# The end of a two-layer encoder: token tile 2 scaled by ScalarE and sent by an adding transfer, a smaller descriptor scratch, five loads on GpSimd's queue

## The chip, the cores and the metric

The kernel runs on one core of one Trainium2 chip, as one program. The metric is the device time of one execution in microseconds (us), lower is better. The engines are called as in the profile: PE (TensorE), DVE (VectorE), ACT (ScalarE), POOL (GpSimd) and SP (SyncE, which here only issues transfers). 16 DMA engines move data; two queues feed them, one issued by SyncE and one by GpSimd.

## The reference

Two layers (DEPTH = 2) over 512 tokens of width 1024, all in float32. Each layer has a token part (a 2-D neighbourhood attention, a bidirectional retention, gates) and a channel part; the end of the program is the end of the second layer's channel part:

```python
for i in range(DEPTH):
    proj = x @ w_in[i]
    q_na, k_na, v_na, q_r, k_r, v_r, g_r, gate_a, gate_b = jnp.split(proj, IN_SPLITS, axis=-1)
    ya = neighbourhood_attention(q_na, k_na, v_na, na_rpb[i])
    yb = bidirectional_retention(q_r, k_r, v_r, g_r, ret_decay_f[i], ret_decay_b[i])
    merged = jax.nn.sigmoid(gate_a) * (ya @ w_branch_a[i]) + jax.nn.sigmoid(gate_b) * (yb @ w_branch_b[i])
    x = layer_norm(DEEPNORM_ALPHA * x + merged @ w_out[i], ln1_g[i], ln1_b[i])
    ffn = conv_glu_ffn(x, w_up[i], conv_w[i], conv_b[i], w_down[i])      # (gelu(a) * b) @ w_down
    ple = jax.nn.sigmoid(x @ w_ple_gate[i]) * (p[i] @ w_ple_proj[i])
    x = layer_norm(DEEPNORM_ALPHA * x + ffn + ple, ln2_g[i], ln2_b[i])

def layer_norm(x, g, b):
    mu, var = mean(x), mean(square(x - mu))          # over the 1024 channels
    return (x - mu) * lax.rsqrt(var + LN_EPS) * g + b
```

## The kernel before

**Precision and weights.** Every matrix product is made of three products of float32r parts (`hi` and `lo` of each operand: `hi*hi`, `hi*lo`, `lo*hi`, in `mm3`). Weights lie in HBM as chunks of 128 x 1024 and pass through one stream (`Stream`): a load into `raw` on SyncE's queue, a cast to `hi` on ScalarE and a subtraction to `lo` on VectorE (`split`), a few chunks ahead of TensorE. Many products are block products in which seven products (`a`, `c`, `t1`, `t2`, `d`, `t3`, `t4`, a Strassen form) replace eight; their weight sums are formed in memory by adding transfers on GpSimd's queue (`Stream.add`, a DMA with `accum_op=add`, into the tiles `rawa` and `rawt`). GpSimd does little else.

**Order.** Nearly everything is kept in the order in which the program is written, on every engine and queue. The stream of a layer is written out by hand: `VG0` and `VG1` are the orders of the first part of layer 0 and 1 (two blocks of retention values and gates, `0a` to `0t4` and `1a` to `1t4`, with the chunks `ga0` to `ga5` of one gate between them), then `FILL` (the heads' `q`, `k`, `nq`, `nk` and others, among them the blocks `2a`, `3a`, `2c`, `3c` at its start), between which the steps of the retention and attention heads are placed. In layer 0, the loads of five constant tables (`cos_sb`, `sin_sb`, `xi_sb`, `dist_sb`, `ident`) are issued at the entry `0t4`, and those of the mask, the bias windows and the convolution weights at `1t4` (`TABLES_AT`). `q_head` (in `FILL`) uses `dist_sb` and `xi_sb` first, in `decays` (L791 to L795).

**Channel part and end.** `pg` forms the gated per-layer input and begins the up-projection; then three segments (`SEGS = (3, 4, 4)`) follow, each with its up-tiles (`up_step`) and the block product of the down-projection. In the last segment of layer 1 (`fin and last`) the layer norm and the output lie between the products. The four token tiles `R[0]` to `R[3]` (128 tokens x 1024) take different ways out:

- Tiles 0 and 1: `out` is filled ahead of time with the layer norm's `b` (a transfer that repeats one row of `ln_par`, on SyncE's queue, before the channel part), and the tile, times `g` and the reciprocal deviation, is added to it in memory by an adding transfer on GpSimd's queue (`send`). Tile 0 is scaled by ScalarE and multiplied by `g` on GpSimd (`norm_gb`), tile 1 by VectorE and ScalarE (`norm_g`, `norm_gs`).
- Tiles 2 and 3: `norm_g` and `norm_b`, both on VectorE, the second with `b` from SBUF (`lnb`), then plain transfers on SyncE's queue; tile 3 goes in two halves of 512 channels.

The reciprocal deviation comes from GpSimd (`rstd_of`, a power), but for tile 3, where ScalarE takes a square root and VectorE and ScalarE make one Newton step (`refine`), so that no engine has to wait for GpSimd. All engines' operations here are in the order of the program: `product("t3")`, the copies `w` of its two results by ScalarE, the ways out of tiles 0 and 1, the additions `into` tiles 2 and 3, `product("t4")` with tile 2's half first, the moments of tiles 2 and 3, `norm_g(2)`, and at last

```python
                if last:
                    norm_b(2, (slice(0, 1024),))
                    refine(3)
                    norm_g(3)
                    norm_b(3, (N1, N2))
```

`unit_f` and `unit_r` take tiles out of one pool of 27 buffers of 4 KB a partition; a tile waits until an earlier one in its buffer is done with. `g` and `b` of the last layer norm (`lng`, `lnb`, by `ln_consts`) are two of them.

Of the kernel before, what the change touches and what calls it, by code (L numbers as in the profile page):

```python
# [10 lines left out]
AF = mybir.ActivationFunctionType  # L11
ALU = mybir.AluOpType
AX = mybir.AxisListType

P = 128
D = 1024
# [5 lines left out]
LN_EPS = 1e-5  # L22
# [3 lines left out]
RPB_N = 8 * 15 * 31  # L26

N_UNIT = 27
N_RAW = 3
N_W = 3  # L30
N_TMP = 6
# [5 lines left out]
XT_HELD = (("t3",), ("t3", "t4"))  # L37
DEEP = 5

FILL = ('2a', '3a', '2c', '3c', 'q0', '2t1', '3t1', 'k0', '2t2', '2d', '3d', '3t2', '2t3', '3t3', '2t4', '3t4', 'k1', 'q1', 'nq0', 'k2', 'nk0', 'q2', 'nk1', 'q3', 'k3', 'nq1', 'nq3', 'nq2', 'nk2', 'nk3', 'vn', 'bb0', 'bb1', 'bb2', 'ga6', 'bb3', 'ga7', 'bb4', 'bb5', 'bb6', 'bb7', 'xn')  # L40
# [5 lines left out]
VG0 = ('p0', 'p1', '0a', '0c', '1a', '1c', 'ga0', '0t1', 'ga1', '0t2', 'ga2', '0d', '0t3', '1t1', '0t4', 'ga3', '1t2', 'ga4', '1d', '1t3', 'ga5', '1t4')  # L46
# [56 lines left out]
def trunk(tc, wpack, x_nat, x_tr, head, p_tr, rpb, decay, ln_par, ln_col, conv, cos_t, sin_t, dist, xi_d, zd, mask, ident_d, out):  # L103
    nc = _Engines(tc)
# [3 lines left out]
    with ExitStack() as es:  # L108
        pool = lambda name, bufs, **k: es.enter_context(tc.tile_pool(name=name, bufs=bufs, **k))
        cp = pool("const", 1)  # L110
        up = pool("unit", N_UNIT)
        xp = pool("xt", 1)
        rp = pool("raw", N_RAW)
        wp = pool("wsplit", N_W)
# [24 lines left out]
        def small(s, n):  # L139
            return sp.tile([P, n], F32, tag=f"s{n}", name=nm(s))  # L140
# [77 lines left out]
        def fill_items(l):  # L218
            by = {}

            for b in range(2, 4):
                pos = {(q, 0): (l, 36 + 4 * (b - 2) + i, 0, 1024) for i, q in enumerate("acbd")}
                for it in block_items(pos, {}, VG_EARLY, 1):
                    by[f"{b}{it.kind}"] = [it]
            return [it for k in FILL for it in (by[k] if k in by else plain_items(l, k))]

# [214 lines left out]
                s3 = ps.rearrange("p (k c) -> p k c", c=P)  # L441
                split(xt[:, 4 * h:4 * h + 4, 0, t * P:(t + 1) * P], xt[:, 4 * h:4 * h + 4, 1, t * P:(t + 1) * P], s3)

        def ln_consts(l, which):
            g = unit_f("lng")
            b = unit_f("lnb")
            nc.sync.dma_start(g, ln_par[l, 2 * which:2 * which + 1, :].to_broadcast([P, D]))
            nc.sync.dma_start(b, ln_par[l, 2 * which + 1:2 * which + 2, :].to_broadcast([P, D]))
            return g, b

        def ln_tile(z, st, g, b, parts):
# [62 lines left out]
        p0 = ws.seq[0]  # L514
# [121 lines left out]
        for l in range(DEPTH):  # L636
# [258 lines left out]
            qn, kn, kl, vn = {}, {}, {}, {}  # L895
# [125 lines left out]
            xn = []  # L1021
# [44 lines left out]
            u, v, keep = {}, {}, {}  # L1066
# [101 lines left out]
            for m in range(8):  # L1168
# [12 lines left out]
                u = unit_r("mt")  # L1181
# [34 lines left out]
            last = l == DEPTH - 1  # L1216

            _Ordered.on = set(ORD)

            if last:  # L1220

                for t in range(2):
                    nc.sync.dma_start(out[t * P:(t + 1) * P, :], ln_par[l, 3:4, :].to_broadcast([P, D]))

            R = [unit_f("R") for _ in range(4)]
            for t in range(4):
                nc.sync.dma_start(R[t], rscr[l][t * P:(t + 1) * P, :])
# [18 lines left out]
            a11, k2, sa, sb, sums = {}, {}, {}, {}, []  # L1246
# [132 lines left out]
            pg()  # L1379
            st = [sp.tile([P, 2, 6], F32, tag="bn", name=nm("bn")) for _ in range(4)]  # L1380
            for s, n in enumerate(SEGS):
                for j in range(tile - 2 * sum(SEGS[:s]), 2 * n):
                    up_step(j, j == 2 * n - 1)
                    residual()
                fin = s == len(SEGS) - 1
# [39 lines left out]
                    if fin:  # L1425
                        nc.vector.bn_stats(st[t][:, cb, :], R[t][:, (N1, N2)[cb]])

                if fin and last:
                    g2c, b2c = ln_consts(l, 1)
                if fin and not last:  # L1430

                    gb = cp.tile([P, 2, 8], F32, name="gb")
# [2 lines left out]
                mv, rs, nmr = {}, {}, {}  # L1435

                def moments(t):
                    mv[t] = small("mv", 2)
                    nc.vector.bn_aggr(mv[t], st[t])
                    if fin and last and t == 3:  # L1440
                        ve[0] = small("ve", 1)
                        nc.vector.tensor_scalar_add(ve[0], mv[t][:, 1:2], LN_EPS)
                        ve[1] = small("sd", 1)
                        nc.scalar.activation(ve[1], ve[0], AF.Sqrt)
                        return
                    rs[t] = rstd_of(mv[t][:, 1:2], LN_EPS, 1)

                ve = {}

                def refine(t):  # L1450

                    r, a, rs[t] = (small(k, 1) for k in ("ri", "ra", "rstd"))
                    nc.vector.reciprocal(r, ve[1])
                    nc.vector.scalar_tensor_tensor(a, r, ve[0], r, op0=ALU.mult, op1=ALU.mult)
                    nc.scalar.activation(a, a, AF.Copy, scale=-0.5, bias=1.5)
                    nc.scalar.activation(rs[t], r, AF.Copy, scale=a)

# [79 lines left out]
                product("t3", u, False)  # L1537
                if fin and last:

                    nc.scalar.copy(w[0], u[0])  # L1540
                    norm_gb(0)
                    nc.scalar.copy(w[1], u[1])
                    norm_gs(1)
                    x4 = u
                elif fin:
                    for i in range(2):
                        norm(i)
                        nc.sync.dma_start(scr[i * P:(i + 1) * P, :], R[i])
# [12 lines left out]
                for k in BOUND if not last else ("t4a", "t4b"):  # L1561
                    if k[0] == "p":
                        ple_half(l + 1, int(k[1]))
                    elif k == "tr":
                        ws.xw = None
                        xt = xp.tile([P, 8, 2, 512], F32R, tag="xt", name=nm("xt"))
                        xf = {}
                        drain(out_pair(0, xt, xf))
                    else:
                        i = "ab".index(k[2]) + 2  # L1570
                        next(t4)
                        into(i, N1, x4[i - 2])
                        stats(i, 0)
                        moments(i)
                        if not last:
                            norm(i)
                            nc.sync.dma_start(scr[i * P:(i + 1) * P, :], R[i])
                        elif i == 2:
                            norm_g(2)
                if last:  # L1580
                    norm_b(2, (slice(0, 1024),))
                    refine(3)
                    norm_g(3)
                    norm_b(3, (N1, N2))
# [128 lines left out]
```

## Time and profile before

| | before |
|---|---|
| median of 3 runs | 1687.07 us |
| lowest, highest | 1686.46, 1687.68 us |
| the profiled execution: its own time | 1687.74 us |
| its span (first to last instruction) | 1686.0 us |
| granted TensorE clock | 0.998 |
| transfers, mean over the span | 170 GB/s |

The page of the profile gives busy time, share of the span and instructions of each engine, and the chain of waits that ended last. Rows of a timeline give start in us, duration in us, engine, line, operation, `out<-in` with the tile names, shape and count, and in brackets the idle time of the engine ahead of it with what ended it. Rows of DMA issues give the count, KB of each and the median time from issue to landing. `SPq` and `POOL ... DMA_DIRECT2D` are issues of transfers on SyncE's and GpSimd's queues. The first and last microseconds of the span are the program's start and its closing barrier.

### The profile page before, as it was taken

The page shows a single profiled execution, that of the slowest core. Times are in us where ns is not written, and L with a number is a line of the kernel's source. Part 1 is how long each engine was busy: PE and PEld are TensorE (multiplying, and loading weights), DVE is VectorE, ACT ScalarE, POOL GpSimd, SP SyncE. Part 2 cuts the span into 40 slices and gives each one's busy share as a digit, 9 for nine tenths or more (in the row PEclk, how much of TensorE's full clock was granted, in tenths as well). Part 3 has the DMA queues.
Part 4 walks back from the last instruction along what each step waited for, and adds up shares of the span by engine and source line. Part 5 has one row for each costly group of instructions (what it writes and reads, how often), then busy time and mean ns, then how long its engine had stood idle before and what let it go on. Part 6 is the DMA issues. An engine that isn't in the chain of part 4 may idle for free.

```text
span 1686.0 us, 21792 instructions
## 1 busy us (share of the span) xinstructions
PE 1672.7 (99%) x8183; PEld 1413.7 (84%) x8183; DVE 1218.7 (72%) x1848; ACT 935.7 (55%) x1400; POOL 177.9 (11%) x204
## 2 busy tenths in 40 slices
PE   9999999999999999999999999999999999999997
PEld 7889988888888888888888898888888888888885
DVE  6746777766787767767876467878588887676678
ACT  6755667773366435344476556586634574453453
POOL 1111111100200100000112011110002010000012
PEclk9999999999999999999999999999999999999999
DMA  8978665666755535536779677656767564274275
GB/s 302 262 190 224 160 145 129 174 175 218 207 137 162 122 113 160 139 105 177 201 221 224 167 201 166 142 129 159 209 245 203 130 168 120 87 200 114 87 212 100
DMA packets 85929, 285.99 MB, mean 170 GB/s; under 512 B 9920, under 2 KB 12480, under 8 KB 85824
## 3 DMA queue, kind: packets, MB, share of 16 engines
q1 hardware_dynamic: 61920, 199.66, 33.7%
q0 software_dynamic: 23904, 84.95, 29.1%
q8 instruction: 64, 1.05, 0.2%
q14 instruction: 41, 0.34, 0.1%
HBM read 265.69 MB, written 17.83 MB: 168 GB/s over the span
## 4 chain that ended last, share of the span: by engine, by line
PE 97%; DVE 1%; ACT 1%; issue 0%; DVEq 0%; ACTq 0%
PE gt L86 32%; PE u L86 13%; PE v L86 7%; PE gt L383 6%; PE gt L384 6%; PE gt L385 6%; PE w L86 4%; PE gn L385 2%; PE gn L383 2%; PE gn L384 2%; PE x L86 1%; PE gn L86 1%; PE u L385 1%; PE u L384 1%; PE u L383 1%; PE na L1005 1%
## 5 line engine op out<-in xcount | busy, mean ns | idle before, releaser
L86 PE MATMUL gt<-x1t,hi 128*128 128x512 f32 x1408 | 433.5, 389 | 0.0
L86 PEld LDWEIGHTS gt<-x1t,hi 128*128 128x128 f32 x1408 | 264.3, 188 | 54.9
L86 PE MATMUL gt<-x1t,lo 128*128 128x512 f32 x704 | 274.1, 389 | 0.1
L86 DVE TENSOR_TENSOR lo<-raw,hi 128x1024 fp32r<-128x1024 f32 (+1 forms) x152 | 181.9, 1207 | 44.4 <-ACT hi L86 44.3
L86 DVE SCALAR_TENSOR_TENSOR ca<-gt,cw,ca 128x511 f32<-128x511 f32 x176 | 131.8, 749 | 78.3 <-ACT ca L86 75.2
L86 ACT CAST hi<-raw 128x1024 fp32r<-128x1024 f32 (+1 forms) x152 | 156.2, 1037 | 36.0 <-PE x L86 11.3
L86 PEld LDWEIGHTS gt<-x1t,lo 128*128 128x128 f32 x704 | 132.1, 188 | 28.2 <-DVE lo L86 1.0
L86 DVE TENSOR_TENSOR lo<-rawa,hi 128x1024 fp32r<-128x1024 f32 x94 | 109.6, 1177 | 52.1 <-ACT hi L86 51.8
L86 ACT ACTIVATE ca<-gt,cw 128x512 f32<-128x512 f32 x88 | 68.5, 779 | 131.6 <-PE gt L86 131.6
L86 ACT CAST hi<-rawa 128x1024 fp32r<-128x1024 f32 x94 | 94.1, 1013 | 36.4 <-DMA rawa<-in_wpack 16.5
L383 PE MATMUL gt<-xt,hi 128*128 128x512 f32 x288 | 113.6, 394 | 0.0
L384 PE MATMUL gt<-xt,hi 128*128 128x512 f32 x288 | 112.3, 390 | 0.0
L385 PE MATMUL gt<-xt,lo 128*128 128x512 f32 x288 | 112.2, 390 | 0.0
L86 POOL DMA_DIRECT2D rawa<-in_wpack x72 | 64.4, 908 | 410.2 <-DVE lo L86 344.2
L341 ACT CAST hi<-raw 128x1024 fp32r<-128x1024 f32 x48 | 50.5, 1052 | 61.0 <-PE gt L384 55.5
L156 ACT CAST hi<-raw 128x1024 fp32r<-128x1024 f32 x43 | 44.9, 1050 | 64.9 <-PE gt L384 34.4
L343 POOL DMA_DIRECT2D lo<-in_wpack x48 | 42.2, 879 | 325.0 <-ACT lo L342 246.8
L157 DVE TENSOR_TENSOR lo<-raw,hi 128x1024 fp32r<-128x1024 f32 x43 | 52.3, 1222 | 16.9 <-ACT hi L156 16.3
L385 PEld LDWEIGHTS gt<-xt,lo 128*128 128x128 f32 x288 | 54.1, 188 | 11.6
L383 PEld LDWEIGHTS gt<-xt,hi 128*128 128x128 f32 x288 | 54.2, 188 | 10.1
L384 PEld LDWEIGHTS gt<-xt,hi 128*128 128x128 f32 x288 | 54.2, 188 | 10.0
L86 PE MATMUL gt<-xt,hi 128*128 128x512 f32 x192 | 59.1, 389 | 0.0
(349 smaller groups left out, 4030.7 us busy)
## 6 DMA issues: line engine op xcount, KB each, us to landing
raw<-in_wpack SPq DMA_DIRECT2D x239, 512.0 KB, 3.7
rawa<-in_wpack POOLq DMA_DIRECT2D x78, 512.0 KB, 6.5
lo<-in_wpack POOLq DMA_DIRECT2D x48, 512.0 KB, 5.5
rawa<-in_wpack SPq DMA_DIRECT2D x26, 512.0 KB, 6.5
rawt<-in_wpack SPq DMA_DIRECT2D x26, 512.0 KB, 6.6
rawt<-in_wpack POOLq DMA_DIRECT2D x26, 512.0 KB, 7.4
r_scr<-pp SPq DMA_DIRECT2D x8, 512.0 KB, 10.0
g_scr<-sga SPq DMA_DIRECT2D x16, 256.0 KB, 3.9
```

The lines of the kernel that those rows point to most:

```text
L86: r = f(*a, **k)
L156: nc.scalar.copy(hi, src)
L157: nc.vector.tensor_sub(lo, src, _f(hi))
L341: nc.scalar.copy(hi[:, cs], it.raw[:, cs])
L343: nc.gpsimd.dma_start(lo[:, cs], wpack[l, c][:, o:o + w], accum_op=ALU.add)
L383: nc.tensor.matmul(ps, lh, rh, start=start, stop=False, skip_group_check=more)
L384: nc.tensor.matmul(ps, lh, rl, start=False, stop=False, skip_group_check=more)
L385: nc.tensor.matmul(ps, ll, rh, start=False, stop=stop, skip_group_check=more)
L1005: nc.tensor.matmul(ov[kt], lv, pt[kt // 2][:, sp_, c], start=i == 0 and sp_ == 0, stop=i == 3 and sp_ == 1)
```

## The change

Token tile 2 now leaves like tile 1: `norm_g` on VectorE, its reciprocal deviation by `refine` (square root on ScalarE, two small operations on VectorE, two on ScalarE), the scaling by ScalarE and an adding transfer on GpSimd's queue. So three rows of tiles of `out` are filled with `b` ahead of time instead of two, and VectorE's second pass over tile 2 is gone. Both copies `w` by ScalarE come before tile 0's way out. The fills of `out` move from SyncE's queue ahead of the channel part to GpSimd's queue at the start of the second segment, and `lng` and `lnb` from SyncE's queue after the last up-tiles to GpSimd's queue at the start of the third. The program's scratch for transfer descriptors is set to 4096 bytes of each partition. In the stream of layer 0, `0t4` (and with it the five tables) moves from ahead of `ga3` to behind `ga5`; in `FILL`, `nq1` and `k3` change places in both layers.

```diff
+SCRATCH = 4096
-FILL = (... 'nk1', 'q3', 'k3', 'nq1', 'nq3', ...)
+FILL = (... 'nk1', 'q3', 'nq1', 'k3', 'nq3', ...)
-VG0 = (... '0d', '0t3', '1t1', '0t4', 'ga3', '1t2', 'ga4', '1d', '1t3', 'ga5', '1t4')
+VG0 = (... '0d', '0t3', '1t1', 'ga3', '1t2', 'ga4', '1d', '1t3', 'ga5', '0t4', '1t4')
...
-        def ln_consts(l, which):
+        def ln_consts(l, which, eng=nc.sync):
             g = unit_f("lng")
             b = unit_f("lnb")
-            nc.sync.dma_start(g, ln_par[l, 2 * which:2 * which + 1, :].to_broadcast([P, D]))
-            nc.sync.dma_start(b, ln_par[l, 2 * which + 1:2 * which + 2, :].to_broadcast([P, D]))
+            eng.dma_start(g, ln_par[l, 2 * which:2 * which + 1, :].to_broadcast([P, D]))
+            eng.dma_start(b, ln_par[l, 2 * which + 1:2 * which + 2, :].to_broadcast([P, D]))
             return g, b
...
-            if last:
-                for t in range(2):
-                    nc.sync.dma_start(out[t * P:(t + 1) * P, :], ln_par[l, 3:4, :].to_broadcast([P, D]))
             R = [unit_f("R") for _ in range(4)]
...
             for s, n in enumerate(SEGS):
+                if last and s == 1:
+                    for t in range(3):
+                        nc.gpsimd.dma_start(out[t * P:(t + 1) * P, :], ln_par[l, 3:4, :].to_broadcast([P, D]))
+                if last and s == 2:
+                    g2c, b2c = ln_consts(l, 1, nc.gpsimd)
                 for j in range(tile - 2 * sum(SEGS[:s]), 2 * n):
                     up_step(j, j == 2 * n - 1)
...
-                if fin and last:
-                    g2c, b2c = ln_consts(l, 1)
...
                 def moments(t):
                     mv[t] = small("mv", 2)
                     nc.vector.bn_aggr(mv[t], st[t])
-                    if fin and last and t == 3:
-                        ve[0] = small("ve", 1)
-                        nc.vector.tensor_scalar_add(ve[0], mv[t][:, 1:2], LN_EPS)
-                        ve[1] = small("sd", 1)
-                        nc.scalar.activation(ve[1], ve[0], AF.Sqrt)
+                    if fin and last and t > 1:
+                        ve[t] = small("ve", 1), small("sd", 1)
+                        nc.vector.tensor_scalar_add(ve[t][0], mv[t][:, 1:2], LN_EPS)
+                        nc.scalar.activation(ve[t][1], ve[t][0], AF.Sqrt)
                         return
                     rs[t] = rstd_of(mv[t][:, 1:2], LN_EPS, 1)
...
                 def refine(t):
                     r, a, rs[t] = (small(k, 1) for k in ("ri", "ra", "rstd"))
-                    nc.vector.reciprocal(r, ve[1])
-                    nc.vector.scalar_tensor_tensor(a, r, ve[0], r, op0=ALU.mult, op1=ALU.mult)
+                    nc.vector.reciprocal(r, ve[t][1])
+                    nc.vector.scalar_tensor_tensor(a, r, ve[t][0], r, op0=ALU.mult, op1=ALU.mult)
                     nc.scalar.activation(a, a, AF.Copy, scale=-0.5, bias=1.5)
                     nc.scalar.activation(rs[t], r, AF.Copy, scale=a)
...
                 product("t3", u, False)
                 if fin and last:
-                    nc.scalar.copy(w[0], u[0])
+                    for i in range(2):
+                        nc.scalar.copy(w[i], u[i])
                     norm_gb(0)
-                    nc.scalar.copy(w[1], u[1])
                     norm_gs(1)
...
                         elif i == 2:
                             norm_g(2)
+                            refine(2)
+                            norm_gs(2)
                 if last:
-                    norm_b(2, (slice(0, 1024),))
                     refine(3)
                     norm_g(3)
                     norm_b(3, (N1, N2))
...
-    nc = bacc.Bacc("TRN2", target_bir_lowering=False, num_devices=1)
+    nc = bacc.Bacc("TRN2", target_bir_lowering=False, num_devices=1, dynamic_dma_scratch_size=SCRATCH)
```

`norm_gs(t)`, not changed, is `R[t] = R[t] * rs[t]` on ScalarE and then `send(t)`, the adding transfer `out[t] += R[t]` on GpSimd's queue.

More of the change, by code (lines that the diff above doesn't have):

```diff
@@ L38 @@
 DEEP = 5
-FILL = ('2a', '3a', '2c', '3c', 'q0', '2t1', '3t1', 'k0', '2t2', '2d', '3d', '3t2', '2t3', '3t3', '2t4', '3t4', 'k1', 'q1', 'nq0', 'k2', 'nk0', 'q2', 'nk1', 'q3', 'k3', 'nq1', 'nq3', 'nq2', 'nk2', 'nk3', 'vn', 'bb0', 'bb1', 'bb2', 'ga6', 'bb3', 'ga7', 'bb4', 'bb5', 'bb6', 'bb7', 'xn')
+FILL = ('2a', '3a', '2c', '3c', 'q0', '2t1', '3t1', 'k0', '2t2', '2d', '3d', '3t2', '2t3', '3t3', '2t4', '3t4', 'k1', 'q1', 'nq0', 'k2', 'nk0', 'q2', 'nk1', 'q3', 'nq1', 'k3', 'nq3', 'nq2', 'nk2', 'nk3', 'vn', 'bb0', 'bb1', 'bb2', 'ga6', 'bb3', 'ga7', 'bb4', 'bb5', 'bb6', 'bb7', 'xn')
 RET_AT = (15, 19, 23, 27)
@@ L44 @@
 RESIDENT = {(l, c) for l in range(DEPTH) for c in range(68, 72)}
-VG0 = ('p0', 'p1', '0a', '0c', '1a', '1c', 'ga0', '0t1', 'ga1', '0t2', 'ga2', '0d', '0t3', '1t1', '0t4', 'ga3', '1t2', 'ga4', '1d', '1t3', 'ga5', '1t4')
+VG0 = ('p0', 'p1', '0a', '0c', '1a', '1c', 'ga0', '0t1', 'ga1', '0t2', 'ga2', '0d', '0t3', '1t1', 'ga3', '1t2', 'ga4', '1d', '1t3', 'ga5', '0t4', '1t4')
 VG1 = ('0a', '0c', '1a', '1c', '0t1', 'ga1', 'ga0', '0t2', 'ga2', '0d', '0t3', '1t1', '0t4', 'ga3', '1t2', 'ga4', '1d', '1t3', 'ga5', '1t4')
```

## The prediction

> **What bounds the kernel now.** I read the page first, then who waited for whom, then the timeline of the last 30 us, then busy times by stretch of those microseconds, and last the first 135 us, where the order of the weight stream changes. The page's head and chain:
>
> ```profile
> span 1686.0 us, 21792 instructions
> PE 1672.7 (99%) x8183; PEld 1413.7 (84%) x8183; DVE 1218.7 (72%) x1848; ACT 935.7 (55%) x1400; POOL 177.9 (11%) x204
> PE 97%; DVE 1%; ACT 1%; issue 0%; DVEq 0%; ACTq 0%
> ```
>
> TensorE is busy for 1672.7 of 1686.0 us. All of its waits, by engine and line, are these two rows:
>
> ```profile
> PE warm L486 <- DVE warm L483: 1.2, 1, 1.2
> PE ns L968 <- DVE kl L928: 0.5, 2, 0.3
> ```
>
> So between the start and the last product nothing but 0.5 us can be won; the change adds and removes no matmul (6968 rows on PE before and after, some in another order). What is left is the stretch behind the last matmul. The timeline of the end, by engine (start in us, duration; the rest as in the page). TensorE:
>
> ```profile
> 1663.46 5.60 PE L86 MATMUL u<-xw,sb 128*128 128x512 f32 x24
> 1668.90 5.60 PE L86 MATMUL u<-xw,k 128*128 128x512 f32 x24
> ```
>
> ScalarE:
>
> ```profile
> 1667.74 0.57 ACT L86 COPY w<-u 128x512 f32<-128x512 f32 x1 [6.78 <-PE u L86]
> 1668.22 0.30 ACT L86 ACTIVATE nmr<-mv,rstd 128x1 f32<-128x1 f32 x1
> ...
> 1669.94 0.58 ACT L86 COPY w<-u 128x512 f32<-128x512 f32 x1
> 1670.45 1.15 ACT L86 ACTIVATE R<-R,rstd 128x1024 f32<-128x1024 f32 x1
> ...
> 1676.70 0.20 ACT L86 ACTIVATE sd<-ve 128x1 f32<-128x1 f32 x1 [3.80 <-DVE ve L86]
> ```
>
> VectorE:
>
> ```profile
> 1674.82 0.68 DVE L86 TENSOR_TENSOR R<-R,u 128x512 f32<-128x512 f32 x1
> ...
> 1676.59 1.28 DVE L86 SCALAR_TENSOR_TENSOR R<-R,rstd,lnb 128x1024 f32<-128x1024 f32 x1
> 1677.79 0.16 DVE L86 RECIPROCAL ri<-sd 128x1 f32<-128x1 f32 x1
> 1677.98 0.22 DVE L86 SCALAR_TENSOR_TENSOR ra<-ri,ve 128x1 f32<-128x1 f32 x1
> 1678.12 1.28 DVE L86 SCALAR_TENSOR_TENSOR R<-R,mv,lng 128x1024 f32<-128x1024 f32 x1
> ```
>
> And the transfers into `out`, by the queue that issues them (GpSimd's are adding, SyncE's plain), with the landing times of SyncE's from the table of DMA issues:
>
> ```profile
> 1672.83 1.81 POOL L86 DMA_DIRECT2D out<-R  x2 [0.30 <-POOL R L86]
> ```
>
> ```profile
> 1677.90 3.38 SPq L86 DMA_DIRECT2D out<-R  x3
> ```
>
> ```profile
> out<-R SPq DMA_DIRECT2D x1, 512.0 KB, 5.8
> out<-R SPq DMA_DIRECT2D x2, 256.0 KB, 4.0
> ```
>
> The last matmul ends at 1668.90 + 5.60 = 1674.5; the remaining 11.5 us are the layer norm of token tiles 2 and 3 on VectorE and five transfers into `out`: tiles 0 and 1 as adding transfers on GpSimd's queue from 1672.83, tile 2 and the halves of tile 3 as plain ones on SyncE's, the last issued near 1680.9 (1677.90 + 3.38 less one issue) and landed 4.0 us later, at 1684.9. The chain of waits follows VectorE here, and it seems that a shorter chain on VectorE is a shorter kernel. The transfers themselves are shown by busy times by stretch (columns: PE, PEld, DVE, ACT, POOL busy, clock, share of the 16 DMA engines, GB/s):
>
> ```profile
> 1673.00:1674.00 1.00, 1.00 (x6) 0.84 (x5) 0.93 (x4) 0.00 (x0) 1.00 (x2) 1.00 0.00 0
> 1676.00:1680.00 4.00, 0.00 (x0) 0.00 (x0) 3.79 (x8) 0.70 (x3) 0.00 (x0) 0.77 1.05 197
> 1680.00:1683.00 3.00, 0.00 (x0) 0.00 (x0) 0.92 (x2) 0.00 (x0) 0.00 (x0) 0.50 0.94 350
> 1683.00:1685.00 2.00, 0.00 (x0) 0.00 (x0) 0.00 (x0) 0.00 (x0) 0.00 (x0) 0.50 0.06 24
> ```
>
> The DMA engines stand idle until 1674, are then full without a gap until 1683, first at 197 GB/s (only adding transfers can be under way: the first plain one is issued at 1677.90), then at 350 GB/s (mostly plain ones). That is the reading on which this forecast rests: the end is set as much by what the DMA engines must move as by VectorE's chain.
>
> **The change part by part.** *VectorE's chain.* Tile 2's last pass (1.28 us at 1676.59) goes. It hid the square root of tile 3: the root ends at 1676.70 + 0.20 = 1676.9, but the reciprocal starts only at 1677.79. In its place two small operations for tile 2 come ahead of the addition at 1674.82; by the same two for tile 3 (1677.79 to the next operation at 1678.12) they take 0.33 us. The root of tile 3 then ends at 1677.23, and the reciprocal gains 1677.79 - 1677.23 = 0.56 us. ScalarE's new scaling of tile 2 costs 1.15 us by the same operation on tile 1; started after the two small ones, it ends near 1677.0, just before ScalarE is needed for that root, so I count it as nothing; if it is late, the gain shrinks by as much. With this gain alone, tile 3's halves would be issued 0.56 us sooner.
>
> *The start of the adding transfers.* Both copies `w<-u` now stand ahead of `nmr`. The second needs the product that ends at 1663.46 + 5.60 = 1669.06, so it starts near 1669.1 and ends at 1669.7. `nmr` started 0.09 us before the end of the copy ahead of it (1667.74 + 0.57 against 1668.22); it now starts at 1669.6 instead of 1668.22, 1.37 us later. Behind it in order stand tile 0's scaling, GpSimd's product with `lng`, and the first adding transfer, which so moves from 1672.83 to 1674.2. The copy that is moved up lets VectorE add tile 3's second half earlier, but VectorE then waits for TensorE's last product anyway: nothing gained. DMA engines that stood idle until 1674 now stand idle until 1675.4.
>
> *Tile 2 as an adding transfer.* It is issued near 1677.1, behind two that are still being moved. 512 KB at 197 GB/s are 2.66 us, at 350 GB/s 1.50 us: 1.16 us more work for engines that are full. Bounds: nothing, if it fits beside the others; above, the distance of the two landings of before,
>
> ```profile
> DMA to landing us min/median/max: 5.6/7.3/9.0
> ```
>
> (out of the stretch with GpSimd's two alone: issued at 1672.8 and 1673.4 by the same view, so landed at 1678.4 and 1682.4): 4.0 us, and 4.0 - 1.5 = 2.5 us more. I take 1.16, because it is a mean over 16 engines, where a landing is the slowest engine's.
>
> The Trainium skill (DMA: Bandwidth & Descriptors, section "Anatomy of one DMA — SWDGE (gpsimd) path") gives a transfer from GpSimd as 2.0 us plus its bytes over 436 GB/s, an estimate of 3.2 us for 512 KB. By it the third would land at 1680.3, ahead of tile 3's halves, and the gain of 0.56 us would be the result. The rows above disagree: 5.6 us for the first, 9.0 for the second. The measurement decides.
>
> *The five loads on GpSimd's queue.* Three rows of `out` and the two of `lng`, `lnb` leave SyncE's queue. GpSimd's queue is empty for long at both new places:
>
> ```profile
> 1492.06 0.86 POOL L86 DMA_DIRECT2D rawt<-in_wpack  x1 [82.89 <-DMA rawt<-in_wpack]
> ...
> 1617.17 0.86 POOL L86 DMA_DIRECT2D rawt<-in_wpack  x1 [87.96 <-DMA rawt<-in_wpack]
> ```
>
> Three issues of 0.86 us in 82.9 us of idle time, and two in 88.0: nothing. What would be queued behind them are the adds for `rawt`; if `lng`'s buffer came free only after 1617, they would be late, and TensorE with them. But the buffer is released by products that stand ahead of that place.
>
> *The scratch.* Two adding transfers of the last stretch are 288 packets on the queue:
>
> ```profile
> q0 software_dynamic: 288, 1.05, 45.6%
> ```
>
> or 9 for each of 16 engines and transfer. By the Trainium skill (SBUF — State Buffer, section "SBUF size: 192, 224, or 256?", and DMA: Bandwidth & Descriptors, its list of terms) the scratch was 16 KiB of each partition and a descriptor is 16 bytes; an estimate from both is room for 113 such transfers before and 28 after. No run here shows it. In the rows of GpSimd above issues stand 80 us apart or few together, and each lands within 9.0 us, so fewer than ten are ever under way: nothing.
>
> *The stream of the first layer.* `0t4` moves behind `ga5`, and the tables tied to it (`dist_sb` among them) with it; the swap of `nq1` and `k3` may take or leave the 0.5 us of `kl`. I count 0.25 us of gain. Rows that bear on `dist_sb` and its first user:
>
> ```profile
> 71.28 0.43 SPq L86 DMA_DIRECT2D dist_sb<-in_dist  x1
> ...
> 120.87 0.33 SPq L86 DMA_DIRECT2D g_scr<-sga  x1
> ```
>
> ```profile
> 125.61 0.41 DVE L791 TENSOR_SCALAR wx<-dist_sb,nlg 128x384 f32<-128x384 f32 x1
> ...
> 129.56 1.23 DVE L157 TENSOR_TENSOR lo<-raw,hi 128x1024 fp32r<-128x1024 f32 x1 [1.07 <-ACT hi L156]
> ```
>
> ```profile
> 134.12 0.28 PE L383 MATMUL w<-xt,hi 128*128 128x256 f32 x1
> ```
>
> ```profile
> dist_sb<-in_dist SPq DMA_DIRECT2D x1, 192.0 KB, 9.6
> out<-in_ln_par SPq DMA_DIRECT2D x2, 512.0 KB, 13.6
> ```
>
> In the new order the five tables are issued right behind `ga5`'s `g_scr`, which comes one product (5.4 us: 24 matmuls) earlier, at 115.4; `dist_sb` is the fourth of them, four issues of some 0.43 us on, so at 117.2, and lands 9.6 us later at 126.8, 1.2 us after VectorE wants it (125.61). Behind it in VectorE's order stands the split `lo` of chunk 3c, done at 130.8 before, and TensorE needs it at 134.12. 3.3 us of cover against 1.2 us: nothing.
>
> **Sum.** The last landing moves by +1.37 + 1.16 = +2.5 us; VectorE's 0.56 us then lies beside the transfers and counts nothing; -0.25 us from `kl`: +2.3 us. The profiled execution took 1687.74 us, its span 1686.0 and 1.7 us around it, and stands 0.67 us above the median of 1687.07. In its last stretch (share 0.06: one engine of sixteen) a single DMA engine lagged for up to 2 us, which I take for that excess. So the +2.3 us go on the median: 1689.4 us.
>
> **The rivals.** (1) *Slower, by the tables.* If `dist_sb` lands 13.6 us after its issue, as the pre-filling of `out` did, VectorE resumes at 130.8, 5.2 us late, and TensorE stalls by what is over the 3.3 us of cover: 1.9 us, in all 1691.3 us. It decides from a landing of 11.7 us on (9.6 us and the 2.1 us of cover left). For it: two weight chunks and the mask are issued right behind the tables. Against: the five tables take the place of nothing urgent, and a chunk's split has 3.3 us to spare. (2) *The third adding transfer is hidden*, the skill's case: VectorE's chain ends last, and the time is 1687.07 - 0.56 - 0.25 = 1686.3 us. For it: the chain of waits runs over VectorE. Against: the DMA engines full for 9 us. (3) *The smaller scratch makes GpSimd wait for room*: if each transfer at the end had to land before the next, three of 5.6 us from 1674.2 end at 1691.0 instead of 1684.9, and the time is 1693 us. (4) *The upper bound of the third transfer*: +1.37 + 2.5 - 0.25, 1690.7 us.
>
> **How the numbers follow.** A measurement of this kernel can tell about 0.2% (3.4 us) from no change. My forecast (the transfers end last, 1688.0 to 1690.7 with rival 4 as its upper end) gets 0.62, of which 0.14 lie above 1690.4; the tables 0.14; the hidden transfer 0.18; the scratch 0.03; a gain over 3.4 us, for which no row has room (11.5 us behind the last matmul, of which a landing alone takes 4 to 5.8), 0.03. Within 0.2%: 0.62 - 0.14 + 0.18 = 0.66. Slower: 0.14 + 0.14 + 0.03 = 0.31. Faster: 0.03. A range from 1686.2 to 1690.9 holds the forecast, its upper end and the hidden transfer, and leaves out 0.20.
>
> **What would show it.** Right: GpSimd's first transfer into `out` near 1674.2 and its third near 1677.1; the third landing after tile 3's halves or with them, 2 to 3 us later than the last landing of before; the DMA engines full from 1675.5 to 1685; the reciprocal of tile 3 near 1677.2; two waits of TensorE or fewer. Wrong: a wait of TensorE between 125 and 140 us (tables), GpSimd's issues far over 0.87 us (scratch), or a last landing that belongs to SyncE's queue before 1684.5 (hidden).

## The result, and the profile after

| | before | changed |
|---|---|---|
| median, same chip | 1686.80 us (19 runs) | 1690.94 us (19 runs) |
| lowest, highest | 1685.84, 1688.47 us | 1689.61, 1691.99 us |
| profiled execution, own time | 1687.74 us | 1690.93 us |

The changed kernel is slower by 4.14 us; the ratio is 1.0023 (95% interval 1.0016 to 1.0031). The forecast was 1689.4 us in a range up to 1690.9; the measured time lies 0.04 us above that end. Its direction held, its size did not: 4.1 us instead of 2.3 us (2.6 over this median of before). That is 0.25% by the medians (the interval begins at 0.16%), the case "Slower" of the prediction, which had 0.31.

Note where the profiled execution of before stands: 0.94 us above its own median, while the changed kernel's stands on its median. The difference of the two traces (3.2 us) is therefore smaller than that of the medians, and in what follows medians price things and traces show mechanisms. The last matmul of before is not late in that execution (it ends at 1674.5 us; in the six other profiled kernels that keep the old order, at 1674.0 to 1675.1), so its excess lies in the end, and where a later trace is set beside that of before, up to 0.9 us of a difference may be this.

The page of the changed kernel, and its waits of TensorE:

```profile
span 1689.1 us, 21783 instructions
PE 1673.1 (99%) x8183; PEld 1414.0 (84%) x8183; DVE 1217.1 (72%) x1849; ACT 938.4 (56%) x1404; POOL 180.9 (11%) x209
```

```profile
PE ns L969 <- DVE kl L929: 0.5, 2, 0.3
PE w L386 <- DVE lo L158: 0.2, 1, 0.2
```

Both pages count 8183 matmuls on PE, so none came or went; the prediction's 6968 is a figure of neither page. The third wait is new. The wait for `kl`, of which 0.25 us were to be gained, is as it was. With the new wait and 0.4 us more of busy time on PE, for which no row shows a cause, the last matmul ends at 1675.1 instead of 1674.5:

```profile
1669.47 5.60 PE L87 MATMUL u<-xw,k 128*128 128x512 f32 x24
```

The timeline of the end, ScalarE, then GpSimd's and SyncE's transfers into `out`:

```profile
1668.32 0.57 ACT L87 COPY w<-u 128x512 f32<-128x512 f32 x1 [6.80 <-PE u L87]
1669.67 0.57 ACT L87 COPY w<-u 128x512 f32<-128x512 f32 x1 [0.79 <-PE u L87]
1670.16 0.30 ACT L87 ACTIVATE nmr<-mv,rstd 128x1 f32<-128x1 f32 x1
```

```profile
1674.75 1.81 POOL L87 DMA_DIRECT2D out<-R  x2 [0.30 <-POOL R L87]
1677.97 0.86 POOL L87 DMA_DIRECT2D out<-R  x1 [1.41 <-ACT sd L87]
1680.53 1.14 SPq L87 DMA_DIRECT2D out<-R  x2
```

The first send is at 1674.75 instead of 1672.83. Of these 1.92 us 0.58 are the later last matmul; the other 1.34 are the second copy, which keeps `nmr` until 1670.16. The landings, from the tables of DMA issues of two stretches of the end:

```profile
out<-R POOLq DMA_DIRECT2D x1, 512.0 KB, 9.2
out<-R SPq DMA_DIRECT2D x2, 256.0 KB, 6.7
```

The third adding transfer lands 9.2 us after 1677.97, at 1687.1, and tile 3's halves, issued no later behind the last matmul than before, take 6.7 us instead of 4.0 and end at 1687.8 (before 1685.0). The stretches show why (PE, PEld, DVE, ACT, POOL busy, clock, share of the 16 DMA engines, GB/s):

```profile
1676.00:1680.00 4.00, 0.00 (x0) 0.00 (x0) 3.42 (x8) 2.31 (x6) 1.42 (x2) 0.80 1.03 162
1680.00:1683.00 3.00, 0.00 (x0) 0.00 (x0) 1.16 (x2) 0.00 (x0) 0.00 (x0) 0.50 1.06 180
1683.00:1685.00 2.00, 0.00 (x0) 0.00 (x0) 0.00 (x0) 0.00 (x0) 0.00 (x0) 0.50 0.99 216
1685.00:1687.50 2.50, 0.00 (x0) 0.00 (x0) 0.00 (x0) 0.00 (x0) 0.00 (x0) 0.50 0.54 191
```

The engines are full from 1676 to 1686, two to three microseconds later than before, and until 1685 at 160 to 220 GB/s; before had 350 from 1680 to 1683. What they had to do, as the share of 30 us (1660 to 1690) by queue, before and then changed:

```profile
q0 software_dynamic: 288, 1.05, 21.3%
q1 hardware_dynamic: 432, 1.05, 8.9%
```

```profile
q0 software_dynamic: 436, 1.57, 30.7%
q1 hardware_dynamic: 288, 0.52, 4.7%
```

Every engine spends 9.2 us on GpSimd's three transfers instead of 6.4 on two (about 3 us each), and 1.4 on SyncE's instead of 2.7 (tile 2's plain one took 1.3). Net, the adding transfer costs 2.8 - 1.3 = 1.6 us of each engine (unrounded 2.82 - 1.26), where the forecast had 1.16.

The last rows are SyncE's waits at the end of the program, before and changed (total, times, longest):

```profile
SPq L1709 <- DMA out<-R: 3.3, 4, 1.1
SPq L1709 <- DMA out<-R: 6.0, 1, 6.0
```

Before, SyncE saw the landings one by one; now it sits in the first wait until the end and takes all the others behind it: from the last landing to the end of the span it is 1.34 us instead of 1.02.

So the 3.2 us between the two traces are 0.6 us until the last matmul's end, 2.3 us more from there to the last landing (12.7 us instead of 10.5; forecast 2.5), and 0.3 us of closing.

### The profile page after: what moved, and what is told of

Read it like the earlier page. It is cut to its first block, busy times and chain, and to the rows that moved or that the text cites. A ratio compares the mean times of both kernels' runs of the same rounds, so it can differ in the third digit from the quotient of the medians.

```text
span 1689.1 us, 21783 instructions
## 1 busy us (share of the span) xinstructions
PE 1673.1 (99%) x8183; PEld 1414.0 (84%) x8183; DVE 1217.1 (72%) x1849; ACT 938.4 (56%) x1404; POOL 180.9 (11%) x209
## 4 chain that ended last, share of the span: by engine, by line
PE 96%; DVE 1%; ACT 1%; DMA 1%; issue 0%; SPq 0%; DVEq 0%; ACTq 0%
PE gt L87 32%; PE u L87 13%; PE v L87 7%; PE gt L384 6%; PE gt L385 6%; PE gt L386 6%; PE w L87 4%; PE gn L386 2%; PE gn L384 2%; PE gn L385 2%; PE x L87 1%; PE gn L87 1%; PE na L1006 1%; PE u L386 1%; PE u L385 1%; PE u L384 1%
## 5 line engine op out<-in xcount | busy, mean ns | idle before, releaser
L386 PEld LDWEIGHTS gt<-xt,lo 128*128 128x128 f32 x288 | 54.1, 188 | 11.5
L385 PEld LDWEIGHTS gt<-xt,hi 128*128 128x128 f32 x288 | 54.2, 188 | 10.1
```

Source lines behind the costliest of these rows:

```text
L385: nc.tensor.matmul(ps, lh, rl, start=False, stop=False, skip_group_check=more)
L386: nc.tensor.matmul(ps, ll, rh, start=False, stop=stop, skip_group_check=more)
```

## The experiments

All times over before are differences of medians taken together on the same chip; the changed kernel's is +4.14 us. In brackets stand the ratio to before and its 95% interval, which reaches some 1.5 us to either side. "Come back" is 4.14 us less the time over before. The intervals of one, two, three, four and six overlap that of the changed kernel, and those of five, eight and ten lie clear of it: prices of single parts are those of medians, with the traces beside them.

**One: the copies in their old place.**

```diff
-                    for i in range(2):
-                        nc.scalar.copy(w[i], u[i])
-                    norm_gb(0)
+                    nc.scalar.copy(w[0], u[0])
+                    norm_gb(0)
+                    nc.scalar.copy(w[1], u[1])
                     norm_gs(1)
```

> The changed kernel with one part undone: the second copy w<-u stands behind tile 0's scaling again, as before. Theory (the DMA engines' work sets the end, and it starts when the first adding transfer is issued): the first transfer into out is issued 1.3 us sooner, behind the last matmul's end by what it was before, the last landing comes 1.3 us sooner, and the time is 1.3 us under the changed kernel's (2.8 us over before). Rival (VectorE's chain for tile 3 sets the end): the time stays at the changed kernel's, 4.1 us over before. Rival (the third adding transfer's issue at 1677.97 sets the end, behind which it takes 9 us whatever the engines did before): the same, no gain.

Measured: 1688.69 us, +2.01 (ratio 1.0012, 1.0003 to 1.0021). 2.1 us come back: the theory's mechanism, and more than its 1.3 us. All eleven times (1688.17 to 1689.61 us) lie at or under the lowest of the changed kernel's. In the trace the first send is 1.7 us ahead of the last matmul's end (1673.83 against 1675.5), as before, and tile 3's halves land 4.2 us after their issue instead of 6.7. The third adding transfer is issued 2.8 us behind the last matmul (2.9 in the changed kernel) and lands after 6.2 us instead of 9.2, so the second rival fell with the first.

**Two: tile 2 plain, as before.**

```diff
-                            refine(2)
-                            norm_gs(2)
...
+                    norm_b(2, (slice(0, 1024),))
                     refine(3)
...
-                    for t in range(3):
+                    for t in range(2):
...
-                    if fin and last and t > 1:
+                    if fin and last and t == 3:
```

> The changed kernel with one part undone: tile 2 is scaled by VectorE and sent by a plain transfer on SyncE's queue, as before; only two tiles of out are pre-filled; the two copies w<-u stay ahead of tile 0's scaling. Theory (DMA work): 1.2 to 1.6 us less of it on every one of 16 engines, and the time is that much under the changed kernel's (2.5 to 2.9 us over before). Rival (VectorE's chain sets the end): it gets 0.6 us longer again, and the time is 0.6 us over the changed kernel's. Rival (the loss lies ahead of the last matmul): no change.

Measured: 1689.09 us, +2.41 (1.0015, 1.0006 to 1.0024): 1.7 us come back, as the 1.6 us of packet time say. In the trace the last landing is 10.3 us behind the last matmul instead of 12.7. VectorE's chain got longer again (its last issue 6.6 us behind the last matmul instead of 6.1) and it did not matter.

**Three: the old order of the first layer.**

```diff
-FILL = (... 'q3', 'nq1', 'k3', 'nq3', ...)
+FILL = (... 'q3', 'k3', 'nq1', 'nq3', ...)
-VG0 = (... '1t1', 'ga3', '1t2', 'ga4', '1d', '1t3', 'ga5', '0t4', '1t4')
+VG0 = (... '1t1', '0t4', 'ga3', '1t2', 'ga4', '1d', '1t3', 'ga5', '1t4')
```

> The changed kernel with the old order of the first layer's products and of the filling products (0t4 ahead of ga3, with the tables behind it near 71 us; k3 ahead of nq1). Theory: the wait of TensorE for w at 134 us goes (0.2 us by the waits, and up to 0.5 us by the time at which the last matmul ends), and the time is 0.3 to 0.6 us under the changed kernel's. Rival (the order is neutral, and the 0.5 us at the last matmul are a run's scatter): no change within 0.1%. Rival (the change moves transfers whose later cost the trace does not show as a wait): more than 1 us.

Measured: 1690.28 us, +3.60 (1.0021, 1.0012 to 1.0030): 0.5 us come back. That is far within the intervals, but the wait for `w` is gone from the trace; it is there in five of the seven profiled kernels with the new order, and in none of the seven with the old one (before included). The last matmul of those with the new order ends at 1675.3 us on average, of those with the old one at 1674.65. Who is late is told by the chain of waits and VectorE's timeline of the changed kernel:

```profile
119.73 11.82 DMA tb<-in_rpb
```

```profile
127.69 0.41 DVE L792 TENSOR_SCALAR wx<-dist_sb,nlg 128x384 f32<-128x384 f32 x1
131.65 0.42 DVE L955 TENSOR_TENSOR B<-tb,mask_sb 128x256 f32<-128x256 f32 x1 [3.54 <-DMA tb<-in_rpb]
133.53 2.49 DVE L158 TENSOR_TENSOR lo<-raw,hi 128x1024 fp32r<-128x1024 f32 x2
```

and by the same rows of before:

```profile
121.77 1.35 SPq L86 DMA_DIRECT2D tb<-in_rpb  x2
```

```profile
125.94 0.42 DVE L954 TENSOR_TENSOR B<-tb,mask_sb 128x256 f32<-128x256 f32 x1
```

It is not `dist_sb` (5.4 us from issue to landing, used at 127.69) but `tb`, the bias window: issued behind five tables, two weight chunks and the mask, it lands after 11.8 us, at 131.55; before it was issued 2.0 us later and landed after 4.0 us, at 125.73. (In the other kernels with the new order it took 11.5 to 12.4 us; in this run, with the old one, 3.8.) VectorE waits 3.54 us for it, and the split of the chunk that TensorE needs stands behind it in VectorE's order. The exchange of `nq1` and `k3` was undone in the same run and not by itself; the wait for `kl` was 0.5 us either way.

**Four: the default descriptor scratch.**

```diff
-    nc = bacc.Bacc("TRN2", target_bir_lowering=False, num_devices=1, dynamic_dma_scratch_size=SCRATCH)
+    nc = bacc.Bacc("TRN2", target_bir_lowering=False, num_devices=1)
```

> The changed kernel without the smaller descriptor scratch (the default instead of 4096 bytes). Theory: no change within 0.1%, because GpSimd's issues took 0.86 us in the changed kernel as before. Rival (the smaller scratch makes GpSimd's descriptors late at the end, where three transfers are queued): 1 us or more under the changed kernel's, with the third transfer's landing sooner than 9.2 us after its issue.

Measured: 1691.99 us, +5.31 (6 runs; 1.0030, 1.0018 to 1.0041): 1.2 us *slower* than the changed kernel, which neither the theory nor the rival had. The smaller scratch is a gain here, and it lies behind the last landing. GpSimd's closing step (DRAIN, the longest of three: the third figure is its duration in ns, and it is the first to start), before, changed, and with the default scratch:

```profile
L1709 POOLq DRAIN  x3: 40/93/11174, 1673.8 to 1685.7; - x3
```

```profile
L1709 POOLq DRAIN  x3: 46/102/10264, 1677.9 to 1688.9; - x3
```

```profile
L1709 POOLq DRAIN  x3: 46/93/10502, 1677.5 to 1688.5; - x3
```

```profile
out<-R POOLq DMA_DIRECT2D x1, 512.0 KB, 7.7
```

Before: it ends at 1673.8 + 11.2 = 1684.9, 2.5 us after GpSimd's last landing (1682.4) and just as SyncE's last transfer lands: hidden. Changed: at 1688.2, 1.07 us after the landing at 1687.1. With the default: at 1688.0, 2.7 us after a landing at 1677.52 + 7.7 = 1685.3; SyncE had been done since 1686.9 and the closing barrier waited 1.1 us. The profiled execution is the fastest of the six (1690.54 us), so its span says nothing of the price; from the last landing to the end of the span it has 2.44 us, the changed kernel 1.34, which is the 1.1 us again.

**Five: both parts of the end undone.** (The edits of one and two together.)

> The changed kernel with both parts of its end undone: the copies w<-u around tile 0's scaling as before, tile 2 by VectorE and a plain transfer, two pre-filled tiles. What stays changed: the order of the first layer, the loads on GpSimd's queue, the scratch. Theory by now (the end is the later of two things, VectorE's chain for tile 3 plus a landing, and the work of the DMA engines; each part alone uses up the slack between them, so that either one undone brought 1.9 to 2.2 us): with both undone no more than 0 to 0.5 us comes on top, so 1688.2 to 1688.8 us, and what is left over before is the order's 0.7 us and up to 1 us more. Rival (two terms that add): 4.1 us under the changed kernel's, the time of before. In the trace, by the theory: the last landing 9.5 to 10.5 us behind the last matmul, as in the kernels with one part undone.

Measured: 1687.68 us, +0.50 (1.0002, 0.9993 to 1.0011). The theory as revised fell; the rival, two terms that add, is right but for the order's 0.5 us: 3.6 us come back, against 2.13 + 1.73 = 3.86. That rests on the medians alone. In the traces the last landing is 10.5 us behind the last matmul, as in before, and 10.3 in one and in two, as if either part undone brought all of the end back. But the profiled execution here is the slowest of its eleven (1689.64 us, 2.0 over their median), with a longer wait for the same `tb`, and that of before stands 0.9 us over its own median, so neither trace shows a usual end.

```profile
PE w L386 <- DVE lo L158: 1.0, 1, 1.0
```

```profile
132.61 0.43 DVE L955 TENSOR_TENSOR B<-tb,mask_sb 128x256 f32<-128x256 f32 x1 [3.56 <-DMA tb<-in_rpb]
```

What stays changed here besides the order, the five loads and the scratch, costs nothing that these medians can tell; the loads were not run by themselves.

**Six: tile 2 on GpSimd's queue, but plain.**

```diff
-                            norm_gs(2)
+                            nc.scalar.activation(R[2], R[2], AF.Copy, scale=rs[2])
+                            nc.gpsimd.dma_start(out[2 * P:3 * P, :], R[2])
```

> The changed kernel, with tile 2's transfer on GpSimd's queue plain instead of adding, so that tile 2 of out lacks lnb; same place, same issue time, same engine. It tells the addition (packets of 328 ns for 4 KB against 159 ns) from the queue. Theory (work of the DMA engines): 16 packets per engine and 0.17 us less for each of 8 descriptors of 4 KB, 1.3 to 1.4 us of every engine, so 1.3 to 1.9 us under the changed kernel's. Rival (what costs is GpSimd's queue: descriptors made late, and its closing step behind the third landing): under 0.4 us gained.

Measured: 1689.24 us, +2.06 (1.0010, 1.0001 to 1.0019): 2.1 us come back, with the same queue, engine and place, no less than with the plain transfer on SyncE's queue (1.7 in two). The trace, of the slowest of the eleven executions (1690.66 us), shows about half of it: GpSimd's packets take 0.9 us less of each engine (25.9% of 32 us against 28.8%), and the last landing comes 11.7 us behind the last matmul instead of 12.7. The addition is what costs; a cost of GpSimd's queue is not seen.

**Seven and eight: tile 1 first**, since it needs no product on GpSimd; in the kernel before (the diff), and in the changed one with the old order, where the same four lines replace the loop.

```diff
                     nc.scalar.copy(w[0], u[0])
-                    norm_gb(0)
+                    norm_gs(1)
                     nc.scalar.copy(w[1], u[1])
-                    norm_gs(1)
+                    norm_gb(0)
```

> The kernel before with one edit: tile 1 (which needs no product on GpSimd) is scaled and sent ahead of tile 0. Theory (the DMA engines, idle until 1674.3, are as late as VectorE's chain): the first transfer into out is issued near 1670.2 instead of 1672.83, the second near 1674.8; the DMA engines are free when tile 3's halves come, and the time is 0.3 to 1.0 us under before. Rival (VectorE's chain alone sets the end of before): the same time as before within 0.2 us. Rival (the copy of u's second bank now comes too late for TensorE's last product): 0.5 us or more over before, with a wait of TensorE for w's copy near 1671.7.

> The changed kernel with the old order of the first layer and with tile 1 scaled and sent ahead of tile 0, the second copy w<-u between the two. Theory: the first adding transfer is issued near 1670.2, the engines move most of the three by 1682.5, and the end is VectorE's chain, which is 0.3 us shorter here than before (last issue 6.1 us behind the last matmul, before 6.4): 1685.8 to 1687.0 us, 0 to 1 us under before. Rival (three adding transfers are too much wherever they start): 1 us or more over before, with the third landing behind tile 3's issue by more than 4.5 us.

Measured: 1687.12 us, -0.06 (0.9997, 0.9988 to 1.0006), and 1688.21 us, +1.03 (1.0006, 0.9997 to 1.0014). Both missed, although the first send was 4.4 us ahead of the last matmul's end. The timeline of seven:

```profile
1672.80 2.39 POOL L86 TENSOR_TENSOR R<-R,lng 128x1024 f32<-128x1024 f32 x1 [1.12 <-ACT R L86]
1674.20 2.06 DVE L86 SCALAR_TENSOR_TENSOR R<-R,mv,lng 128x1024 f32<-128x1024 f32 x1
```

GpSimd's product for tile 0 has moved beside VectorE's product for tile 2, which takes 2.06 us instead of 1.28. VectorE's chain grew by 0.75 us (last issue 7.2 us behind the last matmul instead of 6.4), and now it was the chain that ended last: tile 3's halves land 2.0 us after their issue. In eight VectorE's product took 2.06 us too, and the last issue came 6.8 us behind the last matmul instead of 6.1. By the Trainium skill (SBUF — State Buffer, section "Who interferes with whom") a VectorE instruction with two inputs in SBUF contends with a GpSimd instruction that reads SBUF. The two rows agree: 0.78 us longer.

**Nine and ten: tile 0 scaled early**, in the 6.8 us in which ScalarE waits for the product; in the kernel before (the diff), and in the changed one with the old order.

```diff
+                    norm_gb(0)
                     nc.scalar.copy(w[0], u[0])
-                    norm_gb(0)
-                    nc.scalar.copy(w[1], u[1])
                     norm_gs(1)
+                    nc.scalar.copy(w[1], u[1])
```

> The kernel before with one edit: tile 0 is scaled by ScalarE ahead of both copies w<-u, in the time in which ScalarE waits for TensorE's product (6.8 us of waiting before the first copy); then the first copy, tile 1's scaling, the second copy. GpSimd's product with lng then lies before VectorE's product of tile 2 with lng and not beside it. Theory (the DMA engines' start is one half of the end): both adding transfers are issued 1.4 us sooner (3.1 us ahead of the last matmul's end instead of 1.7), VectorE's chain stays as it was (last issue 6.4 us behind the last matmul), the last landing comes 2.0 to 3.0 us behind that issue, and the time is 0.4 to 1.2 us under before. Rival (VectorE's chain plus a fixed landing sets the end of before): within 0.3 us of before.

> The changed kernel with the old order of the first layer and the same early scaling of tile 0. Theory: the adding transfers start 2.7 us sooner than in the changed kernel, VectorE's product of tile 2 with lng takes 1.3 us again, the last issue comes 6.1 us behind the last matmul, and three adding transfers (2.7 us each from 1.5 us behind the first issue) are done 6.5 to 7.5 us behind it: 0.3 to 1.0 us under before, and level with the kernel before with early scaling. Rival (the third adding transfer costs wherever the others start, because it is issued late itself): 0.5 us or more over before, its landing over 8 us behind the last matmul.

Measured: 1685.94 us, -1.03 (0.9996, 0.9987 to 1.0005), and 1687.48 us, +0.51 (1.0003, 0.9994 to 1.0012). In nine, GpSimd's product does not meet VectorE's as it did in seven, and the sends are 3.2 us ahead of the last matmul's end (1674.0):

```profile
1668.10 2.40 POOL L86 TENSOR_TENSOR R<-R,lng 128x1024 f32<-128x1024 f32 x1
1670.80 1.81 POOL L86 DMA_DIRECT2D out<-R  x2 [0.30 <-POOL R L86]
1673.05 1.28 DVE L86 SCALAR_TENSOR_TENSOR R<-R,mv,lng 128x1024 f32<-128x1024 f32 x1
```

```profile
out<-R SPq DMA_DIRECT2D x2, 256.0 KB, 2.1
```

Tile 3's halves land 2.1 us after their issue (before 4.0, of which some may be the excess of its trace): VectorE's chain ends last. The interval of nine includes no change; the median fits the theory, and eleven, with the same edit, lies under before too. Ten has the same early sends and a chain shorter by 0.4 us (last issue 6.0 us behind the last matmul), and is 1.5 us slower than nine: about the price of the third adding transfer again (ten also has the five loads and the small scratch). Its rows:

```profile
1677.84 0.86 POOL L87 DMA_DIRECT2D out<-R  x1 [4.15 <-ACT sd L87]
```

```profile
out<-R POOLq DMA_DIRECT2D x1, 512.0 KB, 5.4
out<-R SPq DMA_DIRECT2D x2, 256.0 KB, 3.5
```

The third is issued 2.8 us behind the last matmul and takes 5.4 us: 8.2 us. The engines were not free for it, since the second, issued at 1672.55, landed only at 1680.2, and the halves still queue (3.5 us). Here the rival was right.

**Eleven: nine with the small scratch.** `dynamic_dma_scratch_size=4096` added to nine.

> The kernel before with the early scaling and the scratch of 4096 bytes. Theory (GpSimd's closing step lasts 2.5 to 2.7 us behind its last landing with the default scratch and 1.0 to 1.1 with 4096 bytes; with two transfers issued early it ends before SyncE's last landing either way): the same time as with the early scaling alone, within 0.2 us. Rival (the closing step still ends last there): up to 0.7 us under it.

Measured: 1685.61 us, -1.36 (0.9991, 0.9982 to 1.0000). 0.3 us under nine, which is too little to tell the two apart. It is the fastest median of all, with an interval that ends at no change.

**Twelve: 8192 bytes of scratch.** `SCRATCH = 8192` in the changed kernel.

> The changed kernel with a scratch of 8192 bytes instead of 4096. Theory (the closing step of GpSimd's queue clears its descriptor scratch, so that its length goes with the size): it ends 1.4 to 1.8 us behind the third transfer's landing, between the 1.07 us with 4096 bytes and the 2.74 us with the default. Rival (only the default is slow, or the length hangs on something else in these runs): 1.0 to 1.1 us as with 4096, or 2.5 to 2.8 us as with the default.

One execution, 1690.59 us:

```profile
L1709 POOLq DRAIN  x3: 46/102/9937, 1677.7 to 1688.6; - x3
```

It ends at 1687.68, 1.07 us after the third landing (1686.61), exactly as with 4096. The theory that the length goes with the size fell. With 4096 or 8192 bytes it was 0.8 to 1.1 us, with the default 2.5 to 2.7 us; what in the default makes the difference is open.

## Why the prediction was right or wrong

**The reading held.** The DMA engines' work and its start set the end, and VectorE's shorter chain gained nothing. Putting back VectorE's pass over tile 2 (two) made the kernel faster; moving the start alone, in the kernel before, lowered the median by 1.0 us (nine, with an interval that includes no change). The two terms add by the medians (five), as work for engines that are full would; the traces do not show it.

**Start of the sends: right in the trace, small in time.** 1.37 forecast, 1.34 in the trace; undoing it was worth 2.1 us. About 0.5 us of the rest can be seen: by the shares of the queues (27.3% and 4.3% of 32 us) the same transfers took 10.1 us of every engine in one, against 10.6 with the late start. Why late adding packets take longer is open.

**Third adding transfer: the term that was mis-sized.** 1.16 us forecast, from GB/s of two stretches of the timeline. 350 GB/s was the rate of a stretch in which some adding packets still ran beside the plain ones, and 197 that of a stretch well after the adding transfers' start, whose first microsecond moves little at a full share (before):

```profile
1674.00:1675.00 1.00, 0.50 (x3) 0.08 (x1) 1.00 (x2) 0.00 (x0) 1.00 (x2) 1.00 1.03 78
```

By packet time of each queue it is 1.6 us, and the medians price it at 1.7, 2.1 and 1.5 us (two, six, ten against nine), none of them known to better than some 1.5 us. The bounds (0 to 2.5) held it; the value chosen between them was too low.

**Order of the first layer: wrong sign.** -0.25 us forecast, +0.5 by the medians, +0.6 by the ends of the last matmul. The first rival had the mechanism (tables ahead of what is needed sooner) and the wrong victim. It asked when `dist_sb` lands, the one table that moved near to its use; that took 5.4 us, far from the 11.7 at which it would have decided. The step that failed is "the five tables take the place of nothing urgent": the queue behind them was not costed to its end, and `tb` was the last in it. The wait varies from nothing to 1.0 us.

**Scratch: counted at nothing, worth 1.2 us.** The argument that issues do not wait for room was right (0.86 us each, as before). The working looked at issues alone and never at what GpSimd does after the last landing; before, that was hidden to within 0.1 us, so no wait pointed to it. It is a gain only once GpSimd's closing step outlasts SyncE's.

**VectorE's chain.** 0.56 us forecast, 0.34 found: the reciprocal of tile 3 at 1678.03 is 2.95 us behind the last matmul instead of 3.29. Of the missing 0.22 us, about 0.1 lies ahead of the addition for tile 3 (the two small operations took 0.39 us, not 0.33, and VectorE's product before them 1.38, not 1.28), and 0.10 between the end of the root (1677.93) and the reciprocal, which the working had at one moment. Nothing hung on it.

**The rivals.** "Hidden", the case by the Trainium skill (DMA: Bandwidth & Descriptors, section "Anatomy of one DMA — SWDGE (gpsimd) path": an estimate of 3.2 us for 512 KB from GpSimd), fell: 9.2 us, and 5.2 us even for the first adding transfer of seven, which had the engines to itself. "The scratch makes GpSimd wait" fell with the opposite sign. The upper bound of the third transfer, 1690.7, came nearest to the result, for a sum of reasons: start, third transfer and order (2.1 + 1.7 + 0.5, by one, two and three) are 4.3 us, the measured 4.14.

**What was to show it.** Seen: the first send, the third landing beside tile 3's halves, full engines, a last landing 2.8 us later (0.6 of it the later last matmul). Not as forecast: the reciprocal of tile 3 (1678.03, not 1677.2), and a third wait of TensorE at 134.6 us, which the text had named as a sign against it.

## What to carry to other kernels

When the end of a kernel is a burst of transfers, count the busy time of the DMA engines by queue and the moment of the first transfer before shortening any engine's chain; a transfer that adds in memory took 3 us of every engine here where the plain one took 1.3. When loads move in a queue, follow the queue to the last load behind them that somebody waits for, not only the loads that move. And look for idle time of the engine that feeds the first transfer: here one step moved into ScalarE's 6.8 us of waiting lowered the median by 1.0 us, in an interval that includes no change.

## What the runs showed of the hardware that was not expected

- GpSimd's closing step of the program lasts 2.5 to 2.7 us after the last landing on its queue with the default descriptor scratch, and 0.8 to 1.1 us with 4096 or 8192 bytes (the upper figure of each with three adding transfers at the end, the lower ones with two). It shows only in the rows of its sequencer.
- A product of two tiles in SBUF on VectorE (128x1024) took 2.06 us beside GpSimd's product of the same size, and 1.28 us without; GpSimd's took 2.4 us either way.
